# Moving the stores of what ScalarE made from the sync queue to ScalarE's DMA queue

## The chip, the cores and the metric

One core of one Trainium2 chip runs the whole kernel in one launch. The metric is the device time of that launch in microseconds (us). Engines are called as the profile calls them: PE is TensorE, ACT is ScalarE, DVE is VectorE, POOL is GpSimd, SP is SyncE, which here does nothing but issue transfers. SPq and ACTq are the instruction queues of SP and ACT.

## The reference

A bidirectional encoder block over 4096 positions and 1024 channels, in float32, one layer:

```python
xn = rmsnorm(x, norm_g)
proj = xn @ w_in                       # 4608 columns: v, x0, x1, hyena gate, lru in, lru gate
hy = dwconv3(proj[v, x0, x1])          # centred, width 3
u = v * x1
y_hy = x0 * (fftconv(u, kfilt) + skip * u)     # filter from a small sin network
xb = dwconv4(lru_in)
y_lru = rglru(xb, forward) + rglru(xb, backward)
y = concat(rmsnorm(y_hy) * silu(hy_gate), rmsnorm(y_lru) * silu(lru_gate)) @ w_out
out = rmsnorm(x + y, final_g)
```

The FFT convolution is done as matrix products: a first DFT over 128 points of the time index, a second one over 64 with twiddles in it, the product of the two spectra, and the inverse in two steps.

## The kernel before, in words

Every product is three float32r matmuls (high by high, high by low, low by high parts), so PE does most of the work. The input projection (`inproj`, L287) walks 36 blocks of 128 output columns in four passes. Within a pass it walks eight chunks of 512 positions, and each step is 24 matmuls into one of two `mm` banks of PSUM. The normalised input is kept in DRAM as `xs`, and in passes two to four `load_x` (L262) brings each chunk back as eight loads of 512 KB into 12 slots.

`consume` (L359) takes each result off PSUM. The lru input and the v, x0, x1 blocks go through `conv` (ACT and DVE). For x1 the product with v is transposed by PE in `store_u` (L339), ACT copies the result into a slot of `s4`, and a store puts it into `ut_d`: 48 pairs of block and chunk, 60 stores with the split ones at both ends (L348 to L357). A gate block is one SiLU on ACT into a slot of `cv`, and a store into `s_d`: 96 of them (L380).

Other streams are woven between the steps of the projection, in the order filter, scans, convolution:
- `phase_filter` (L473) makes the filter and its first DFT, 64 columns `j`. ACT evacuates each and a store goes to `ef_d` (L532).
- `phase_lru` (L383) loads `xb_d` in tiles of 1024 positions, makes gates (PE, ACT, DVE), scans on DVE, and stores the forward result `yf_d` and the sum `yl_d`.
- `phase_u` (L575) does the first DFT of u: 32 loads, 64 evacuations on ACT, 32 stores into `eu_d` (L600).
- `phase_mid` (L608) runs over 65 frequencies. `load` (L610) brings `ef` and `eu` for one frequency into two slots each, ACT makes the high part and POOL the low part, `tabs` (L618) loads the twiddle tables, `spectrum` multiplies, and `inverse` (L652) of the frequency before makes `r`, which is stored into `ey_d` (64 stores, L658).
- `phase_iy` (L678) does the last inverse step, 32 groups with two stores each into `yt_d` (L706).

Then `phase_out` (L710) loads the gates and branches back, normalises, projects through `w_out` and writes the output. Its tiles reuse the space of the projection's pools.

All tile dependencies become semaphores. The order of instructions in each engine's queue is written at build time by a planner that simulates the program (`schedule_with_timeline_sim=True`, L876). At run time each queue goes strictly in that order: an instruction whose semaphore has not come holds all behind it. Before the change every transfer but four loads of small parameters is issued by SP, loads and stores in one order.

Of the kernel before, what the change touches and what calls it, by code (L numbers as in the profile page):

```python
# [19 lines left out]
P = 128  # L20
L = 4096
# [4 lines left out]
TC = 512  # L26
# [85 lines left out]
def tile_hymba_block(ctx: ExitStack, tc: tile.TileContext, a: dict, out: bass.AP, dbg=None):  # L112
    nc = tc.nc
# [10 lines left out]
    s_d = [dram.tile([2, CB, P, TC], F32, name=f"sd{n}") for n in range(NCH)]  # L124
    ef_d = dram.tile([64, 2, 64, C], F32, name="efd")
    eu_d = dram.tile([64, 2, 64, C], F32, name="eud")
    ey_d = dram.tile([64, 2, 64, C], F32, name="eyd")
# [22 lines left out]
    def aux_ps():  # L150
        return pcfg["pool"].tile([P, 2, 512], F32, name="aux", bufs=pcfg["aux"])
# [29 lines left out]
    def prm(name, i):  # L181
        t, c0 = par[name]
        return t[:, c0 + i:c0 + i + 1]
# [149 lines left out]
    def store_conv(res, dst):  # L333
        y, skip, N, t0 = res
        nc.sync.dma_start(dst[:, t0 + skip:t0 + N], y[:, skip:N])
# [3 lines left out]
    def store_u(b, res):  # L339
        y, skip, N, t0 = res  # L340
        dst = ut_d[:, b * P:(b + 1) * P]
        ps = pcfg["pool"].tile([P, TC], F32, name="tp", bufs=1).rearrange("p (q c) -> p q c", c=P)
        for q in range(4):
            nc.tensor.transpose(ps[:, q, :], y[:, q * P:(q + 1) * P], ident)
        th = xpool.tile([P, 4, P], F32, name="s4", bufs=3)
        nc.scalar.activation(th, ps, AF.Copy)
        if skip:
            nc.sync.dma_start(dst[0:P - 1], th[1:, 0, :])  # L348
            nc.sync.dma_start(dst[P - 1:4 * P - 1].rearrange("(q t) c -> t q c", t=P), th[:, 1:, :])
        else:  # L350
            nc.sync.dma_start(dst[t0:t0 + TC].rearrange("(q t) c -> t q c", t=P), th)
        if N > TC:
            ps = pcfg["pool"].tile([P, TC], F32, name="tp", bufs=1).rearrange("p (q c) -> p q c", c=P)
            nc.tensor.transpose(ps[0:1, 0, :], y[:, TC:TC + 1], ident)
            th = xpool.tile([P, 4, P], F32, name="s4", bufs=3)
            nc.scalar.activation(th[0:1, 0], ps[0:1, 0], AF.Copy)
            nc.sync.dma_start(dst[L - 1:L], th[0:1, 0])  # L357

    def consume(n, e, ps):  # L359
        if 24 <= e < 30:  # L360
            i = e - 24
            store_conv(conv(n, 18 + i, ps, [prm("lcw", 6 * k + i) for k in range(4)], prm("lcb", i)), xb_d[i])
        elif e < 18:
            if 6 <= e < 12:
                r = conv(n, e, ps, [x0w[:, 6 * k + e - 6:6 * k + e - 5] for k in range(3)], x0w[:, 12 + e:13 + e])
            else:
                r = conv(n, e, ps, [prm("hcw", 18 * k + e) for k in range(3)], prm("hcb", e))
            if e < 6:
                hold[e] = r
            elif e < 12:  # L370
                store_conv(r, x0_d[e - 6])
            else:
                y, N = r[0], r[2]
                nc.gpsimd.tensor_tensor(y[:, :N], y[:, :N], hold.pop(e - 12)[0][:, :N], ALU.mult)  # L374
                store_u(e - 12, r)
        else:
            g = xpool.tile([P, TC + 8], F32, name="cv", bufs=3)
            nc.scalar.activation(g[:, :TC], ps, AF.Silu)
            r, i = (0, e - 18) if e < 24 else (1, e - 30)
            nc.sync.dma_start(s_d[n][r, i], g[:, :TC])  # L380


    def phase_lru():  # L383
# [74 lines left out]
    def mm3(ps, lhs, rhs, first=True, last=True):  # L458
        for h in range(2):
            for i, (x, y) in enumerate(((0, 0), (0, 1), (1, 0))):  # L460
                nc.tensor.matmul(ps[:, h, :NH], lhsT=lhs[:, x], rhs=rhs[:, y, h * NH:(h + 1) * NH],  # L461
                                 start=first and i == 0, stop=last and i == 2)
# [4 lines left out]
    def hv(t):  # L467
        return t[:, :, 0:NH]

    def cv2(t):  # L470
        return t.rearrange("p (h c) -> p h c", h=2)

    def phase_filter():  # L473
        with ExitStack() as st:
            hid = []
            for i in range(2):
                t = st.enter_context(tc.tile_pool(name=f"hid{i}", bufs=1)).tile([P, 2048], F32, name=f"hid{i}")
# [42 lines left out]
            for i in range(2):  # L520
                t = fw.tile([P, 2, 64], F32, name=f"lh{i}")
# [5 lines left out]
            ev = ef_d.rearrange("k r j c -> (k r) j c")  # L527
            def first_dft(j, kw, kr):
                ps = aux_ps()
                mm3(ps, fa, kr)  # L530
                nc.scalar.activation(cv2(kw), hv(ps), AF.Copy)
                nc.sync.dma_start(ev[:, j, :], kw)  # L532

            pend = None
            for j in list(range(1, 64)) + [0]:
# [15 lines left out]
                kw = fw.tile([P, C], F32, name="kw", bufs=3)  # L551
# [23 lines left out]
    def phase_u():  # L575
        JB = 2
        with tc.tile_pool(name="uu", bufs=1) as up:
            f0 = up.tile([P, P], F32, name="f0")
            nc.sync.dma_start(f0[0:64], a["c_fa"][0:64])
            nc.sync.dma_start(f0[64:], a["c_fa"][0:64])  # L580
            fu = up.tile([P, 2, P], F32R, name="fu")
            nc.vector.tensor_copy(fu[:, 0], f0)
            nc.vector.tensor_tensor(fu[:, 1], f0, fu[:, 0].bitcast(F32), ALU.subtract)
            ev = eu_d.rearrange("k r j c -> (k r) j c")
            uv = ut_d.rearrange("(p j) c -> p j c", j=64)
            for g in range(64 // JB):
                ui = up.tile([64, JB, C], F32, name="uin", bufs=3)
                nc.sync.dma_start(ui, uv[:, g * JB:(g + 1) * JB, :])
                t = up.tile([P, JB, C], F32R, name="ut", bufs=2)
                nc.vector.tensor_copy(t[0:64], ui)  # L590
                nc.vector.tensor_tensor(t[64:], ui, t[0:64].bitcast(F32), ALU.subtract)
                stg = up.tile([P, JB, C], F32, name="ustg", bufs=3)
                for j in range(JB):
                    ps = aux_ps()
                    for h in range(2):
                        for w in range(2):
                            nc.tensor.matmul(ps[:, h, :NH], lhsT=fu[:, w], rhs=t[:, j, h * NH:(h + 1) * NH],  # L597
                                             start=w == 0, stop=w == 1)
                    nc.scalar.activation(cv2(stg[:, j]), hv(ps), AF.Copy)
                nc.sync.dma_start(ev[:, g * JB:(g + 1) * JB, :], stg)  # L600
                yield WU


# [4 lines left out]
    def phase_mid():  # L608
        with tc.tile_pool(name="mid", bufs=1) as mp:
# [42 lines left out]
            def inverse(terms, s):  # L652
                ps = aux_ps()
                for m, (w, t) in enumerate(terms):
                    mm3(ps, w, t, m == 0, m == len(terms) - 1)
                o = mp.tile([P, C], F32, name="r", bufs=3)
                nc.scalar.activation(cv2(o), hv(ps), AF.Copy)
                nc.sync.dma_start(ey_d[s].rearrange("r j c -> (r j) c"), o)  # L658

            pend = None  # L660
            for k in range(64):
# [16 lines left out]
    def phase_iy():  # L678
        with tc.tile_pool(name="iy", bufs=1) as ip:
            fz = ip.tile([P, 2, P], F32, name="fz")  # L680
            nc.vector.memset(fz, 0.0)
            for i in range(2):
                nc.sync.dma_start(fz[:, i, 64 * i:64 * i + 64], a["c_fi"])
            fi = ip.tile([P, 2, 2, P], F32R, name="fi")
            nc.vector.tensor_copy(fi[:, 0], fz)
            nc.vector.tensor_tensor(fi[:, 1], fz, fi[:, 0].bitcast(F32), ALU.subtract)
            ev = ey_d.rearrange("k r j c -> (k r) j c")
            yv = yt_d.rearrange("(p j) c -> j p c", j=64)
            for g in range(32):
                e = ip.tile([P, 2, C], F32, name="e", bufs=NE)  # L690
                nc.sync.dma_start(e, ev[:, 2 * g:2 * g + 2, :])
                es = ip.tile([P, 2, 2, C], F32R, name="es", bufs=2)
                nc.scalar.activation(es[:, 0], e, AF.Copy)
                nc.vector.tensor_tensor(es[:, 1], e, es[:, 0].bitcast(F32), ALU.subtract)
                ps = aux_ps()
                for h in range(2):
                    m = 0
                    for i in range(2):
                        for fp, ep in ((0, 0), (0, 1), (1, 0)):
                            nc.tensor.matmul(ps[:, h, :NH], lhsT=fi[:, fp, i], rhs=es[:, ep, i, h * NH:(h + 1) * NH],  # L700
                                             start=m == 0, stop=m == 5)
                            m += 1
                o = ip.tile([P, C], F32, name="yo", bufs=3)
                nc.scalar.activation(cv2(o), hv(ps), AF.Copy)
                for i in range(2):
                    nc.sync.dma_start(yv[2 * g + i], o[64 * i:64 * i + 64])  # L706
                yield WI


# [170 lines left out]
```

## Time and profile before

| what | value |
|---|---|
| median of 3 runs | 2980.05 us (2979.57 to 2982.83) |
| the profiled execution's own time | 2983.15 us |
| its span, first to last instruction | 2981.2 us |
| granted TensorE clock, mean | 0.987 of full speed |
| PE busy | 2864.0 us (96%) |
| DVE, ACT, POOL busy | 2023.1, 1763.4, 832.4 us |
| DMA, mean over the span | 198 GB/s, 590.22 MB |

The time is what the runs are compared by. The span is what every other number of the profile is a part of. Busy time of DMA-issuing instructions is counted for no engine; they stand in the queues' own rows (SPq and the like). A wait names who ended it.

### The profile page before, as it was taken

What the parts mean: (1) busy time and instruction counts of PE and PEld (TensorE: products, weight loads), DVE (VectorE), ACT (ScalarE), POOL (GpSimd) and SP (SyncE); (2) the same over time, 40 slices, a digit from 0 to 9 for tenths busy, and PEclk for the clock granted to TensorE, in tenths of its full rate; (3) what the DMA queues carried; (4) which work ended last, traced back from release to release, by engine and by line L of the source; (5) the groups of instructions that cost most, each with busy time, mean ns of one, the idle gap of its engine ahead of it and who ended that gap; (6) DMA issues with size and microseconds to landing.
All of it is one profiled execution on the core that took longest, in us unless ns stands there. A gap on an engine that the chain in (4) does not pass through costs nothing.

```text
span 2981.2 us, 37289 instructions
## 1 busy us (share of the span) xinstructions
PE 2864.0 (96%) x13211; PEld 2390.1 (80%) x13211; DVE 2023.1 (68%) x2024; ACT 1763.4 (59%) x2575; POOL 832.4 (28%) x1012
## 2 busy tenths in 40 slices
PE   8999999999899898999999999999999989999998
PEld 6778888887777676777888788888888868888886
DVE  6987778657696678776666876666733366666665
ACT  4668776658697685987446667666644422222222
POOL 0013234422332323121005667766600010000001
PEclk9999999999999999999999999999999979999999
DMA  7434445434454446555986776666688665455542
GB/s 263 152 136 184 183 167 193 150 126 159 152 178 154 164 152 200 196 200 186 337 313 216 245 263 233 233 238 218 200 293 295 235 220 173 162 167 170 178 160 75
DMA packets 287352, 590.22 MB, mean 198 GB/s; under 512 B 29532, under 2 KB 150320, under 8 KB 286910
## 3 DMA queue, kind: packets, MB, share of 16 engines
q1 hardware_dynamic: 287038, 587.78, 57.2%
q8 instruction: 105, 1.72, 0.2%
q14 instruction: 81, 0.66, 0.1%
q0 software_dynamic: 128, 0.05, 0.0%
HBM read 361.24 MB, written 226.49 MB: 197 GB/s over the span
## 4 chain that ended last, share of the span: by engine, by line
PE 60%; ACT 13%; DVE 10%; DMA 8%; issue 6%; POOL 3%; SPq 1%; ACTq 0%; POOLq 0%; DVEq 0%
PE mm L302 11%; PE mm L304 11%; PE mm L303 11%; PE aux L461 9%; PE aux L785 4%; PE aux L783 4%; PE aux L784 4%; PE aux L700 2%; DMA eu<-eud 2%; DVE cv L330 2%; PE aux L597 2%; DVE sy L762 2%; ACT L433 1%; ACT L421 1%; ACT aa L424 1%
## 5 line engine op out<-in xcount | busy, mean ns | idle before, releaser
L302 PE MATMUL mm<-x,w 128*128 128x512 f32 x2304 | 911.9, 397 | 15.7 <-DMA x<-xs 6.6
L303 PE MATMUL mm<-x,w 128*128 128x512 f32 x2304 | 910.5, 395 | 0.0
L304 PE MATMUL mm<-x,w 128*128 128x512 f32 x2304 | 907.0, 394 | 0.0
L302 PEld LDWEIGHTS mm<-x,w 128*128 128x128 f32 x2304 | 436.0, 189 | 108.6 <-DMA x<-xs 10.0
L304 PEld LDWEIGHTS mm<-x,w 128*128 128x128 f32 x2304 | 435.9, 189 | 85.7 <-issue 0.5
L303 PEld LDWEIGHTS mm<-x,w 128*128 128x128 f32 x2304 | 436.2, 189 | 83.3 <-issue 1.9
L330 DVE SCALAR_TENSOR_TENSOR cv<-raw,cols,cv 128x512 f32<-128x512 f32 (+2 forms) x336 | 270.3, 807 | 117.2 <-ACT cv L328 112.1
L783 PE MATMUL aux<-w,A 128*128 128x512 f32 x768 | 304.7, 399 | 9.9 <-ACT w L728 9.9
L784 PE MATMUL aux<-w,A 128*128 128x512 f32 x768 | 304.7, 397 | 1.4 <-DVE w L729 1.4
L785 PE MATMUL aux<-w,A 128*128 128x512 f32 x768 | 304.7, 400 | 0.0
L764 POOL CAST sr<-sy 128x256 fp32r<-128x256 f32 x32 | 36.4, 1138 | 740.0 <-DVE sy L762 495.2
L615 POOL TENSOR_TENSOR ef<-ef 128x768 fp32r<-128x768 f32 x64 | 125.6, 1962 | 236.2 <-DMA ef<-efd 181.1
L419 PE MATMUL aux<-hl,wg 128*128 128x512 f32 x576 | 156.9, 401 | 24.8 <-DVE hl L412 11.2
L320 ACT ACTIVATE raw<-mm 128x512 f32<-128x512 f32 x192 | 113.5, 591 | 109.7 <-PE mm L304 109.4
L783 PEld LDWEIGHTS aux<-w,A 128*128 128x128 f32 x768 | 145.8, 190 | 40.7 <-ACT w L728 10.6
L374 POOL TENSOR_TENSOR cv<-cv 128x512 f32<-128x512 f32 (+1 forms) x48 | 73.1, 1523 | 369.6 <-DVE cv L330 354.6
L784 PEld LDWEIGHTS aux<-w,A 128*128 128x128 f32 x768 | 145.7, 190 | 34.8 <-DVE w L729 2.9
L785 PEld LDWEIGHTS aux<-w,A 128*128 128x128 f32 x768 | 145.9, 190 | 31.0
L757 ACT ACTIVATE y<-y 128x1536 f32<-128x1536 f32 x32 | 47.7, 1489 | 204.8 <-DVE S L756 187.1
L456 DVE TENSOR_TENSOR rs<-r,rs 128x768 fp32r<-128x768 f32 x65 | 94.5, 1453 | 94.9 <-ACT rs L455 94.9
L419 PEld LDWEIGHTS aux<-hl,wg 128*128 128x128 f32 x576 | 107.6, 190 | 61.3 <-DVE hl L412 17.4
L615 POOL TENSOR_TENSOR eu<-eu 128x768 fp32r<-128x768 f32 x64 | 125.3, 1957 | 30.4 <-ACT eu L614 30.4
(193 smaller groups left out, 5220.0 us busy)
## 6 DMA issues: line engine op xcount, KB each, us to landing
x<-xs SPq DMA_DIRECT2D x192, 512.0 KB
xs<-x SPq DMA_DIRECT2D x64, 512.0 KB
efd<-kw SPq DMA_DIRECT2D x64, 384.0 KB
xb<-xbd SPq DMA_DIRECT2D x48, 512.0 KB
sd<-cv SPq DMA_DIRECT2D x96, 256.0 KB
eud<-ustg SPq DMA_DIRECT2D x32, 768.0 KB
ef<-efd SPq DMA_DIRECT2D x64, 384.0 KB
eu<-eud SPq DMA_DIRECT2D x64, 384.0 KB
```

The costliest lines, as they stand in the source:

```text
L302: nc.tensor.matmul(ps, lhsT=w[:, 0, kt, :], rhs=x[kt][:, 0], start=kt == 0, stop=False)
L303: nc.tensor.matmul(ps, lhsT=w[:, 0, kt, :], rhs=x[kt][:, 1], start=False, stop=False)
L304: nc.tensor.matmul(ps, lhsT=w[:, 1, kt, :], rhs=x[kt][:, 0], start=False, stop=kt == KT - 1)
L320: nc.scalar.activation(R[:, K - 1:K - 1 + TC], ps, AF.Copy)
L330: nc.vector.scalar_tensor_tensor(y[:, :N], R[:, k:k + N], w[k], y[:, :N], op0=ALU.mult, op1=ALU.add)
L419: nc.tensor.matmul(ps[:, h], lhsT=wg[:, u, 2 * d + gi, :], rhs=v[:, hs], start=i == 0, stop=i == 2)
L456: nc.vector.tensor_tensor(dst[:, 1], src, dst[:, 0].bitcast(F32), ALU.subtract)
L461: nc.tensor.matmul(ps[:, h, :NH], lhsT=lhs[:, x], rhs=rhs[:, y, h * NH:(h + 1) * NH], start=first and i == 0, stop=last and i == 2)
L615: eng.tensor_tensor(t[:, 1], raw, t[:, 0].bitcast(F32), ALU.subtract)
L783: nc.tensor.matmul(ps[:, h], lhsT=ht, rhs=w[:, 0, sl], start=b == 0, stop=False)
L784: nc.tensor.matmul(ps[:, h], lhsT=ht, rhs=w[:, 1, sl], start=False, stop=False)
L785: nc.tensor.matmul(ps[:, h], lhsT=lt, rhs=w[:, 0, sl], start=False, stop=b == CB - 1)
```

## The change

The eight store instructions whose source tile was written by ACT are issued with `nc.scalar.dma_start` in place of `nc.sync.dma_start`. The loads, and the stores of what DVE or POOL made, stay on SP. Sizes, slots and arithmetic are the same. The planner orders the queues anew.

```diff
@@ store_u
         if skip:
-            nc.sync.dma_start(dst[0:P - 1], th[1:, 0, :])
-            nc.sync.dma_start(dst[P - 1:4 * P - 1].rearrange("(q t) c -> t q c", t=P), th[:, 1:, :])
+            nc.scalar.dma_start(dst[0:P - 1], th[1:, 0, :])
+            nc.scalar.dma_start(dst[P - 1:4 * P - 1].rearrange("(q t) c -> t q c", t=P), th[:, 1:, :])
         else:
-            nc.sync.dma_start(dst[t0:t0 + TC].rearrange("(q t) c -> t q c", t=P), th)
+            nc.scalar.dma_start(dst[t0:t0 + TC].rearrange("(q t) c -> t q c", t=P), th)
...
-            nc.sync.dma_start(dst[L - 1:L], th[0:1, 0])
+            nc.scalar.dma_start(dst[L - 1:L], th[0:1, 0])
@@ consume
-            nc.sync.dma_start(s_d[n][r, i], g[:, :TC])
+            nc.scalar.dma_start(s_d[n][r, i], g[:, :TC])
@@ phase_filter, first_dft
-                nc.sync.dma_start(ev[:, j, :], kw)
+                nc.scalar.dma_start(ev[:, j, :], kw)
@@ phase_u
-                nc.sync.dma_start(ev[:, g * JB:(g + 1) * JB, :], stg)
+                nc.scalar.dma_start(ev[:, g * JB:(g + 1) * JB, :], stg)
@@ phase_mid, inverse
-                nc.sync.dma_start(ey_d[s].rearrange("r j c -> (r j) c"), o)
+                nc.scalar.dma_start(ey_d[s].rearrange("r j c -> (r j) c"), o)
@@ phase_iy
-                    nc.sync.dma_start(yv[2 * g + i], o[64 * i:64 * i + 64])
+                    nc.scalar.dma_start(yv[2 * g + i], o[64 * i:64 * i + 64])
```

## Rows read from the trace of the kernel before

**Rows 1.** The page, engines: busy us, share of the span, instructions.
```profile
PE 2864.0 (96%) x13211; PEld 2390.1 (80%) x13211; DVE 2023.1 (68%) x2024; ACT 1763.4 (59%) x2575; POOL 832.4 (28%) x1012
```

**Rows 2.** Busy time by stretch: length, busy us of each engine, clock, DMA.
```profile
220.00:690.00 470.00, 470.00 (x2324) 410.18 (x2324) 332.70 (x433) 336.41 (x583) 164.66 (x388) 1.00 0.46 166
690.00:1400.00 710.00, 657.37 (x2843) 525.53 (x2842) 542.46 (x446) 572.49 (x744) 196.64 (x126) 0.98 0.51 175
...
1640.00:2170.00 530.00, 513.92 (x2430) 440.86 (x2429) 380.46 (x344) 358.33 (x477) 356.82 (x353) 1.00 0.68 235
```

**Rows 3.** SP's own waits, 690 to 1400: us in total, times, longest.
```profile
SPq L442 <- DVE bb L441: 154.3, 24, 10.6
...
SPq L351 <- ACT s L346: 61.0, 21, 8.1
...
SPq L380 <- ACT cv L378: 16.6, 7, 5.2
...
SPq L266 <- PE mm L304: 8.8, 19, 2.6
```

**Rows 4.** SP's own waits, 1640 to 2170.
```profile
SPq L658 <- ACT r L657: 108.9, 42, 6.1
SPq L620 <- POOL ib L625: 94.5, 41, 5.1
SPq L380 <- ACT cv L378: 60.3, 30, 4.4
...
SPq L266 <- PE mm L304: 6.4, 15, 1.0
```

**Rows 5.** SP's queue in order of time, 1900 to 1917: start, us.
```profile
1912.99 0.32 SPq L658 DMA_DIRECT2D eyd<-r  x1
1913.41 0.38 SPq L613 DMA_DIRECT2D ef<-efd  x1
```

**Rows 6.** ACT's waits, 1640 to 2170.
```profile
ACT eu L614 <- DMA eu<-eud: 78.3, 37, 6.2
...
ACT ef L614 <- DMA ef<-efd: 34.5, 27, 3.5
```

**Rows 7.** DMA issues from 690 to 1400: count and KB each.
```profile
utd<-s SPq DMA_DIRECT2D x31, 256.0 KB
...
sd<-cv SPq DMA_DIRECT2D x9, 256.0 KB
...
utd<-s SPq DMA_DIRECT2D x5, 0.5 KB
```

**Rows 8.** Two lines' issue instructions: duration in ns, least, median, most.
```profile
L351 SPq DMA_DIRECT2D utd<-s x42: 365/371/797, 150.5 to 1196.7; - x42
...
L380 SPq DMA_DIRECT2D sd<-cv x96: 319/320/924, 1223.4 to 2380.0; - x96
```

**Rows 9.** ACT in order of time, 400 to 440: two neighbours.
```profile
418.56 0.81 ACT L531 ACTIVATE kw<-aux 128x768 f32<-128x768 f32 x1
419.25 0.95 ACT L546 ACTIVATE win<-absd,tn 128x768 f32<-128x768 f32 x1
```

**Rows 10.** The chain that ended last, 690 to 1400, share of it by line.
```profile
by line: issue 12.3%; DVE cv L330 6.1%; ACT L433 5.0%; ACT L421 4.4%; PE mm L302 4.4%; PE mm L304 4.3%; ACT aa L424 4.3%; PE mm L303 4.3%; ACT th L421 4.0%; ACT m L427 4.0%; DMA x<-xs 4.0%; DVE bb L429 3.5%; ACT th L425 3.2%; ACT m L433 3.2
```

**Rows 11.** PE's waits, 690 to 1400.
```profile
PE tp L344 <- POOL cv L374: 13.7, 4, 5.8
PE aux L419 <- DVE hl L412: 11.2, 11, 2.3
...
PE mm L302 <- DMA x<-xs: 6.6, 5, 3.5
```

**Rows 12.** The same chain, two of its transfers: start, us.
```profile
973.40 2.64 DMA yfd<-bb
...
2380.05 5.25 DMA sd<-cv
```

**Rows 13.** SP's own waits over the whole run, one ended by a load.
```profile
SPq L600 <- DMA x<-xs: 8.8, 6, 2.6
```

## The prediction

> **What bounds the kernel now.** I read the engines' busy times first, then the busy times by stretch, and then, for the stretches in which PE isn't full, who waited for whom. PE is busy 96% of the span [rows 1]. The stretches tell where the other 4% are [rows 2]. From 220 to 690 (filter) PE is busy all 470 us. From 1400 to 1640 (first DFT of u) and from 2170 to 2360 (last inverse step) it is the same: full, with no wait of PE listed. No queue order can speed these up; they can only lose. PE idles 52.6 us of the 710 from 690 to 1400 (the scans) and 16.1 us of the 530 from 1640 to 2170 (the middle of the convolution) [rows 2]. So what the change can give sits in these two stretches and at the seam near 2380, where the output phase takes over; what it can cost sits wherever ACT is near full.
>
> What holds the loads is seen in SP's own waits. SP takes its transfers in one fixed order, so a store that waits for ACT keeps back every load behind it. In the middle stretch the longest waits of SP are for ACT's `r` (108.9 us in 42 waits) and, third, for ACT's gate (60.3) [rows 4]. One place shows the pattern: the store of `r` goes out at 1912.99, and the load of `ef` directly behind it, 0.42 us after it starts [rows 5]. ACT in turn idles 78.3 and 34.5 us there for `eu` and `ef` [rows 6].
>
> **Part one: 380 issues leave SP.** By the loops these are 60 + 96 + 64 + 32 + 64 + 64 stores. An issue takes 0.320 us for the gates and 0.371 for the transposed u [rows 8], so at least 380 x 0.320 = 122 us of issuing leave SP. I value this at nothing by itself: SP spends its time in waits, and what covers the issues is the same waits. At worst it stays nothing.
>
> **Part two: loads that stood behind the stores.** In the middle stretch SP's listed waits sum to 321.9 us (seven rows, the first and the last of them shown). Of these 108.9 + 60.3 = 169.2 us, 53%, go away from SP [rows 4]. If the 16.1 us of idle PE [rows 2] fall in proportion, that is -8.5 us. The ends are 0 (the `eu` load stays behind the table load, whose wait for POOL, 94.5 us, stays [rows 4]) and -16.1. I take the proportion, because the `ef` load is the one released.
>
> In the scans SP's listed waits sum to 535.9 us (eleven rows); 61.0 + 16.6 = 77.6 us of them, 14.5%, go [rows 3]. The largest, for the forward scan's `bb`, stays. The waits of PE that begin with late loads are 13.7 (the product on POOL, queued behind loads of `hf`), 11.2 (low part of `xb`) and 6.6 (x) [rows 11], 31.5 us in sum; 14.5% of it is -4.6 us. The ends are 0 and -31.5; the share going is small, so I stay with it.
>
> **Part three: the last gate store.** At the seam the chain runs through the store of the last gate, 5.25 us from issue to landing, behind loads of the output phase on the same queue. A store of twice its size that stood alone took 2.64 us [rows 12]. On a queue of its own I give it that: -2.6 us, with 0 as the other end. [...]
>
> **Part four: what ACT pays.** A store on ACT's queue stands behind the activation that made its data and needs its end. Two neighbours on ACT overlap now: one starts at 418.56 and takes 0.81, the next starts at 419.25, 0.12 us before the first one's end [rows 9]. With a store between them that overlap goes and the issue comes in: 0.320 + 0.12 = 0.44 us for most, 0.371 + 0.12 = 0.49 for u. The trace has no issue on ACT; the nearest rows are these of SP. Below, it could be nothing, where ACT idles behind the store anyway.
>
> In the scans there are 31 + 9 + 5 such stores [rows 7]: 31 x 0.49 + 14 x 0.44 = 21.4 us. ACT is busy 572.49 of 710 us there [rows 2], the fullest it gets in any long stretch, and seven of the entries in the chain are ACT's: 5.0 + 4.4 + 4.3 + 4.0 + 4.0 + 3.2 + 3.2 = 28.1% [rows 10]. So 28.1% of 21.4, +6.0 us; ends 0 and +21.4. Queued behind a held ACT are the tanh and square root of the gates, and DVE's scan waits for these.
>
> In the middle stretch 60 + 51 stores at 0.44 make 48.8 us. I cost this at nothing: ACT idles 78.3 + 34.5 = 112.8 us for loads there [rows 6], more than twice that, and this idle time covers it. Without the cover it costs up to 48.8 us.
>
> In the three full stretches the 64 + 32 + 64 stores and the gates there are covered by PE's own work; ACT is busy 336.41 of 470 us in the first [rows 2]. One cost has no row of ACT: SP's stores sometimes wait for a load that they do not read, 8.8 us in six waits at L600 [rows 13]. So transfers share semaphores, and such a wait would now hold ACT. I take 0, because PE keeps some steps of PSUM ahead; the upper end is four lines at 8.8 us each, +35.
>
> **The sum.** -8.5 - 4.6 - 2.6 + 6.0 = -9.7 us. The profiled execution took 2983.15 us (span 2981.2 and 1.95 around it), so its like would take 2973.5. It lies 3.1 us above the median of the runs, 2980.05, from which the forecast is taken: 2970.4 us. What can be told from no change is about 0.2%, 6 us.
>
> **The rivals.** *ACT becomes the bound.* The holds in the two stretches sum to 21.4 + 48.8 = 70.2 us. The gains of parts two and three sum to 15.7. From 21.7 us of holds on the path (31% of them) the kernel is slower by over 6 us; at half it is +35.1 - 15.7 = +19.4, 2999.5 us. For it: ACT's 81% in the scans [rows 2], and 28% of the chain without any store in it [rows 10]. Against it: the idle time of rows 6.
>
> *Nothing moves.* The loads held by a store were early enough. PE is full in three stretches, and the 16.1 us of the middle come from the products of spectra, not from `ef`. Holds and gains then cancel: 2980, between 2974 and 2986. [...]
>
> The planner's new order can move each case by some microseconds either way; that is why neither gain nor loss gets more than half of the chance.
>
> **How the numbers follow.** Gain: 0.42, at 2970, own range 2954 to 2974 (the lower end has the middle's whole 16.1, the seam's 2.6 and 7 of the scans' 31.5, with holds that cost nothing). Nothing moves: 0.27. ACT as the bound: 0.31, at 2999.5, from 2986 up; the part over 3008 (over 62% of the holds on the path) I give 0.1, below 2954 another 0.07. So the range is 2954 to 3008, and faster, same, slower are 0.42, 0.27, 0.31.
>
> **What would show it.** Right: SP's waits at L351, L380, L532 and L658 gone; `ef` loads issued without a wait for ACT; ACT's waits for `ef` shorter; PE idle in 1640 to 2170 under 10 us; the last gate store landing in under 3.5 us; ACT's idle time in the scans shorter by some 20 us. Wrong: waits of ACT for transfers that its next work does not need, or PE waits for ACT's `th`, `bb` or `cv` growing from 690 on; an order of the projection's steps that differs so much that stretches no longer match.

## The result, and the profile after

The changed kernel takes 3007.3 us in the median of 4 runs (3005.6 to 3011.79), the kernel before on the same chip 2981.31 (2979.57 to 2982.83). The ratio is 1.009, 95% interval 1.0074 to 1.0106: some 27 us slower, where 10 us faster were forecast. The profiled execution's span is 3003.7 us against 2981.2.

The page's engine line of the kernel after. Against [rows 1], ACT gains 1.6 us and PE 5.8, for the same 13211 matmuls, on a span 22.5 longer; the mean granted clock is 0.986 against 0.987. Most of the growth is therefore idle time of PE.

```profile
PE 2869.8 (96%) x13211; PEld 2390.3 (80%) x13211; DVE 2026.2 (67%) x2024; ACT 1765.0 (59%) x2575; POOL 834.3 (28%) x1012
```

The same kernel by stretch, with the columns of [rows 2]. The last line is the kernel before from 1400 to 1640.

```profile
220.00:690.00 470.00, 470.00 (x2326) 410.44 (x2325) 331.97 (x434) 337.96 (x583) 157.32 (x386) 1.00 0.47 167
690.00:1400.00 710.00, 650.81 (x2809) 518.61 (x2808) 532.56 (x440) 569.85 (x738) 203.13 (x125) 0.98 0.51 173
1400.00:1640.00 240.00, 237.58 (x1113) 204.26 (x1113) 151.31 (x136) 113.17 (x196) 35.42 (x37) 1.00 0.80 276
1640.00:2170.00 530.00, 506.70 (x2374) 432.33 (x2373) 388.65 (x344) 359.65 (x480) 364.18 (x357) 0.99 0.66 227
```

```profile
1400.00:1640.00 240.00, 240.00 (x1133) 208.07 (x1132) 156.30 (x140) 120.80 (x206) 40.13 (x42) 1.00 0.83 280
```

PE's idle time grew from 52.6 to 59.2 us in the scans, from 0 to 2.4 from 1400 to 1640, and from 16.1 to 23.3 in the middle of the convolution, by 16.2 us in all. Read the counts beside the busy times. From 220 to 690 nothing is lost (2326 matmuls against 2324). In the scans PE gets through 2809 matmuls where it got through 2843, from 1400 to 1640 through 1113 (1133 before), in the middle of the convolution through 2374 (2430): 34 + 20 + 56 = 110 fewer. Matmuls of the projection follow each other at 0.23 us here (227 ns from start to start, the median of either trace), so that is about 25 us, as an estimate, and the span grew by 22.5. Most of the loss, 90 of the 110, is in the two stretches in which gain was looked for.

PE's waits of the kernel after, 690 to 1400 (us in total, times, longest). Among those that grew against the kernel before are that for `hl` (from 11.2 to 14.2, [rows 11]), that for a gate's `cv` (from 3.0 to 4.8) and that for `bb` (from 1.9 to 3.7). The second fence has the last two of the kernel before.

```profile
PE aux L419 <- DVE hl L412: 14.2, 12, 2.6
...
PE mm L302 <- ACT cv L378: 4.8, 2, 2.4
...
PE aux L419 <- ACT bb L421: 3.7, 10, 1.1
```

```profile
PE mm L302 <- ACT cv L378: 3.0, 1, 3.0
...
PE aux L419 <- ACT bb L421: 1.9, 8, 0.3
```

PE's longest wait from 1640 to 2170 is for the product of spectra (`rs`, made by DVE): first of the kernel after, then of the kernel before.

```profile
PE aux L461 <- DVE rs L456: 10.2, 17, 1.6
```

```profile
PE aux L461 <- DVE rs L456: 6.6, 11, 1.1
```

SP's waits of the kernel after, first 690 to 1400, then 1640 to 2170. The waits at L351, L380 and L658 of [rows 3, 4] are gone as announced. But the time SP waited did not go. All its waits together are 586 us in the scans (567 before) and 425 in the middle (372 before): there the table load's wait for POOL's `ib` alone is 231.7 us, 94.5 before.

```profile
SPq L442 <- DVE bb L441: 170.9, 23, 10.6
SPq L409 <- DVE bb L429: 168.1, 38, 20.6
...
SPq L266 <- PE mm L304: 17.7, 21, 4.6
```

```profile
SPq L620 <- POOL ib L625: 231.7, 45, 9.2
SPq L613 <- PE aux L461: 67.5, 34, 5.7
```

ACT's waits of the kernel after in the middle: both waits for loads are shorter than in [rows 6], by 6.2 and 9.1 us, and PE idles more all the same.

```profile
ACT eu L614 <- DMA eu<-eud: 72.1, 32, 5.2
...
ACT ef L614 <- DMA ef<-efd: 25.4, 12, 3.7
```

ACT and its queue in order of time, after. The gate's activation ends at 1311.55; the store's issue takes 0.33 us; the table load after it starts 0.38 us after that end. With no store between them, the next activation (it ends at 1314.29) and the table load behind it are 0.01 us apart.

```profile
1310.95 0.60 ACT L378 ACTIVATE cv<-mm 128x512 f32<-128x512 f32 x1
1311.58 0.33 ACTq L380 DMA_DIRECT2D sd<-cv  x1
1311.93 1.28 ACT L433 ACT_TABLE_LOAD   x1 [0.39 <-ACT cv L378]
1313.23 1.06 ACT L433 ACTIVATE m<-m 128x1024 f32<-128x1024 f32 x1
1314.30 1.28 ACT L421 ACT_TABLE_LOAD   x1
```

The order of the queues was planned anew, and that is much more than the moved stores. For each engine: the instructions that both programs have in its queue, and the fewest of them that must change place to turn the one order into the other.

```
PE    13179 instructions, 1713 of them change place
DVE    2024                 98
ACT    2358                218
POOL   1012                 92
SP     1250                 79   (the transfers that stay on SP)
```

### The profile page after: what moved, and what is told of

It is laid out like the page before. It is cut to its first block, busy times and chain, and to the rows that moved or that the text cites. A ratio compares the mean times of both kernels' runs of the same rounds, so it can differ in the third digit from the quotient of the medians.

```text
span 3003.7 us, 37110 instructions
## 1 busy us (share of the span) xinstructions
PE 2869.8 (96%) x13211; PEld 2390.3 (80%) x13211; DVE 2026.2 (67%) x2024; ACT 1765.0 (59%) x2575; POOL 834.3 (28%) x1012
## 5 line engine op out<-in xcount | busy, mean ns | idle before, releaser
L764 POOL CAST sr<-sy 128x256 fp32r<-128x256 f32 x32 | 34.5, 1080 | 747.2 <-DVE sy L762 510.2
L419 PE MATMUL aux<-hl,wg 128*128 128x512 f32 x576 | 159.6, 405 | 27.0 <-DVE hl L412 14.2
```

Source lines behind the costliest of these rows:

```text
L419: nc.tensor.matmul(ps[:, h], lhsT=wg[:, u, 2 * d + gi, :], rhs=v[:, hs], start=i == 0, stop=i == 2)
```

## Experiments: the order or the queue

**Order and queue apart.** The theory: the time went into the new order of instructions, above all PE's, and not into the queue. The rival: into the queue, through holds of ACT and shared semaphores. An order can be held: after tracing, an edge without a semaphore is added from each instruction to the next one of a recorded order, so that the planner must write that order. The places of the transfers in the queues of SP and ACT stay the planner's. `ORDER` is the recorded order, as packed numbers of instructions. That a queue runs in its planned order shows in the traces of before and after: numbered by the two recorded orders, ACT's 2358 activations agree one by one in line, tiles and shape.

```diff
+def pin_order(tc, engines):
...
+    info = mybir.DependencyInfo(mybir.DependencyClass.NoSync, mybir.DependencyReason.DATA)
+    for e in engines:
+        names = np.cumsum(np.frombuffer(zlib.decompress(base64.b85decode(ORDER[e])), "<i4")).tolist()
+        for a, b in zip(names, names[1:]):
+            tc.add_manual_dep(traced[b], f"I-{a}", info, reason="order")
...
     with tile.TileContext(nc, schedule_with_timeline_sim=True) as tc:
         tile_hymba_block(tc, args, out)
+        pin_order(tc, ('PE', 'DVE', 'Pool', 'Activation'))
```

First, the kernel before with all stores on SP, its four computing engines held to the changed kernel's order:

> All stores back on SP's queue, but PE, DVE, POOL and ACT work through their instructions in exactly the order that the planner wrote for the changed kernel. Theory A, the planner's new order costs the time: about 3003 us, as slow as the changed kernel (+22 us or more). Theory B, the queue itself costs it (ACT held by its stores, loads and stores that wait for each other's semaphores): about 2981 us, the time of the kernel before.

Then the changed kernel's stores on ACT with the order of the kernel before:

> All 380 stores on ACT's queue as in the change, but PE, DVE, POOL and ACT's activations keep exactly the order of the kernel before, and SP's loads all but exactly. Theory A, the new order: about 2981 us or some microseconds less, since the loads no longer stand behind the stores (the forecast of part two, up to -16). Theory B, the queue itself: 3003 us or more, with waits of ACT behind its own stores in the scans (21 us of holds) and the middle (49 us).

And the same with PE alone held to the order of before (`pin_order(tc, ('PE',))`):

> All stores on ACT's queue; only PE keeps the order of the kernel before, ACT, DVE, POOL and SP have what the planner writes for them with the stores on ACT. Theory A1, PE's own order (how many steps of the projection stand between a frequency's second DFT and its inverse) carries the cost of the new plan: about 2987 us, within 0.2% of before. Theory A2, the orders of ACT and DVE carry it: about 3000 us or more.

| kernel | median us | before, same chip | ratio, 95% interval |
|---|---|---|---|
| order of after, stores on SP | 3004.39 | 2986.72 | 1.0063 (1.0048 to 1.0077) |
| order of before, stores on ACT | 2987.44 | 2986.72 | 1.0002 (0.9992 to 1.0011) |
| PE's order of before, stores on ACT | 2989.64 | 2982.63 | 1.0018 (1.0007 to 1.0029) |

The order alone, without a store moved, costs 0.63%, 19 us by the ratio. All 380 stores on ACT's queue cost nothing that can be told when the order of before is held. PE's order accounts for most: with it alone restored, and the other engines planned around it, 0.9% becomes 0.18%. What is left between 0.63% and 0.9% (1.009/1.0063 = 1.0027, 8 us, the two intervals put together reach from about 1.0005 to 1.0049) belongs to the queue in that order.

The traces hint at where. In the order of after, PE idles 51.8 us in the scans with the stores on SP (the line below) and 59.2 with the stores on ACT; in the middle it is 22.9 and 23.3. So the loss of the middle is there without a moved store, and that of the scans seems to come with the queue. This is one execution of each, and their spans differ by only 2.2 us.

```profile
690.00:1400.00 710.00, 658.19 (x2823) 524.87 (x2822) 534.91 (x442) 572.80 (x741) 203.81 (x125) 0.97 0.50 173
```

The middle stretch, 1640 to 2170, of these three, in the order of the table: PE 507.07 us and 2390 matmuls, as in the kernel after, then 514.49 and 516.42, as before.

```profile
1640.00:2170.00 530.00, 507.07 (x2390) 430.77 (x2389) 386.44 (x347) 357.65 (x478) 367.19 (x359) 1.00 0.66 228
```

```profile
1640.00:2170.00 530.00, 514.49 (x2439) 443.89 (x2438) 385.57 (x348) 362.83 (x481) 363.42 (x356) 0.99 0.68 237
```

```profile
1640.00:2170.00 530.00, 516.42 (x2450) 445.95 (x2449) 388.70 (x351) 365.43 (x486) 367.64 (x359) 0.99 0.68 235
```

The kernel with the order of before and its stores on ACT is the clean test of the change itself. SP's waits in its middle stretch:

```profile
SPq L620 <- POOL ib L625: 181.1, 47, 6.6
SPq L613 <- PE aux L461: 121.2, 46, 7.5
```

The 169.2 us of waits behind stores are gone, and the loads wait for themselves instead: the table load for POOL to be done with the slot (94.5 before), the loads of `ef` and `eu` (both L613) for PE to be done with theirs (23.6 before). The loads that came to the head of the queue sooner met slots that weren't free: these two waits grew from 118.1 to 302.3 us together. ACT's wait for `ef` is halved there, and PE idles 15.5 us against 16.1:

```profile
ACT eu L614 <- DMA eu<-eud: 68.2, 31, 7.3
...
ACT ef L614 <- DMA ef<-efd: 16.2, 10, 3.6
```

**One group of stores at a time, planned freely.** Only the change to L380 is left in the first, only that to L658 in the second.

```diff
-            nc.sync.dma_start(s_d[n][r, i], g[:, :TC])
+            nc.scalar.dma_start(s_d[n][r, i], g[:, :TC])
```

> Only the 96 gate stores on ACT's queue, everything planned anew. PE's order departs from the kernel before after the gates begin (about 1223 us) and the middle's median distance from second DFT to inverse falls from 10.4 to 9.9 us of PE work. Theory A (the order): some 8 us lost from 1200 to 1400 and some 8 in the middle, 2996 to 3003 us. Theory B (holds of ACT by these 96 stores at 0.44 us, up to 42 us of them, a third on the path): the same time, but with ACT's own stores as what PE's waits lead back to; A would show them led back to DVE and to positions in the order.

```diff
-                nc.sync.dma_start(ey_d[s].rearrange("r j c -> (r j) c"), o)
+                nc.scalar.dma_start(ey_d[s].rearrange("r j c -> (r j) c"), o)
```

> Only the 64 stores of the inverse's result on ACT's queue, everything planned anew. The order is that of the kernel before up to the middle stretch, there the median distance falls from 10.4 to 9.7 us of PE work. Theory A: nothing until 1600 us, then some 10 us lost in the middle: about 2992 us. If the order is only a matter of luck and not of this distance: no loss, 2980 to 2986.

The gates alone: 3002.04 us against 2982.63, ratio 1.0059 (1.0045 to 1.0073). The `r` stores alone: 2990.26, 1.0026 (1.0017 to 1.0035). The 96 gate stores, a quarter of those moved, bring two thirds of the loss, and with them 1401 instructions of PE change place, where all the stores move 1713. Of the two losses expected, some 8 us each, the middle's shows (PE idles 25.1 us there, 16.1 before), and that from 1200 to 1400 us only in part (17.4 us against 14.6). As theory A has it, PE's longest wait in the middle leads back to DVE:

```profile
PE aux L461 <- DVE rs L456: 16.2, 24, 1.5
```

The `r` stores lose less than the 10 us expected in the middle (18.8 us of idle PE against 16.1), though their plan has the same median distance, 9.7 us, as the changed kernel. That already speaks against the distance as the cause.

**New plans without a moved store.** Is this loss what the planner does to a store on ACT's queue, or what any new plan does here? Two small shifts of the weave, each with the stores on SP and on ACT. The first also moves one step of the projection over the border of two stretches, so it isn't a new plan alone; the second is nearer to that.

```diff
-X2 = 28
+X2 = 29
```

> All stores on SP as before; X2 is 29 in place of 28, so one step of the projection moves from the convolution's stretch to the scans', and the planner writes a new order. Theory A (the change lost time because its new order happened to be a worse one; the order of the kernel before is a good draw): this order loses too though no queue changed, 2988 to 3005 us, and in the middle stretch more waits of PE for the product of spectra than the 6.6 us before. Theory B (the planner orders badly because it takes a store on ACT for cheap): within 0.2% of the kernel before, 2976 to 2988.

> The same shift of one step, with all the stores on ACT, planned freely. Theory A: another draw, within 0.3% of its twin with the stores on SP (the queue itself gave 0.02% and 0.2% when the order was held). Theory B: slower than its twin by 0.6 to 0.9%, about 3005 us or more.

```diff
-S2 = 1.0
+S2 = 1.01
```

> All stores on SP; the weight of the scans in the weave (S2) is 1.01 in place of 1, which shifts their steps a little against the projection's. Theory A: not the order of before, so slower by 0.2 to 0.8%, 2988 to 3005. Theory B: within 0.2% of the kernel before.

> The same weight with all stores on ACT, planned freely. Theory A: within 0.3% of its twin on SP. Theory B: slower than its twin by 0.6 to 0.9%.

| weave | stores on SP | stores on ACT | ACT over SP |
|---|---|---|---|
| X2 = 29 | 1.0104 (1.0087 to 1.0121) | 1.0126 (1.0111 to 1.0142) | 1.0022 |
| S2 = 1.01 | 1.0023 (1.0013 to 1.0034) | 1.0051 (1.0036 to 1.0066) | 1.0028 |
| as it was | 1 | 1.0090 (1.0074 to 1.0106) | 1.0090 |

Both new plans lose with no queue changed, 0.23% and 1.04% (2988.96 and 3011.28 us against 2983.77). So a plan other than the one of before costs time without a moved store; the 1.04% is as much as the whole change cost, but part of it may be the step that was moved. Theory B of these expectations falls; A holds, save that the first shift costs more than its 2988 to 3005. Each twin on ACT is 0.2 to 0.3% over its twin on SP, the same size as the 0.27% above. The twins' orders differ too, and for the first pair the two intervals put together reach down to no difference.

The middle stretch of the first shift with its stores on SP; it stands beside that of the kernel after, 26 us of PE idle.

```profile
1640.00:2170.00 530.00, 504.08 (x2360) 427.19 (x2359) 388.96 (x343) 356.32 (x476) 366.64 (x355) 0.99 0.66 227
```

**What in the order does it?** In the planned order of before, 10.4 us of PE work (median over the frequencies, by the durations of the traces) lie between a frequency's second DFT and its inverse; in that of the changed kernel 9.7. The theory: too little work there to cover the product on DVE. The edit, made on a held order of PE, keeps the six matmuls of an inverse together and moves them behind the projection's matmuls that follow them. The lines show the pattern of one frequency: `mm` is the projection, `ef` and `eu` the two DFTs, `rs` the inverse. Only PE is held here; the other engines are planned anew around it, and no run holds the changed kernel's own order of PE without the edit.

```diff
-PE: eu x6, mm x10, rs x1, mm x5, rs x5, mm x2, ef x6
+PE: eu x6, mm x10, mm x5, mm x2, rs x6, ef x6
```

> The changed kernel, its stores on ACT, with PE held to the changed kernel's own order but for one edit: in the middle of the convolution the six matmuls of each frequency's inverse are kept together and moved behind the projection's matmuls that follow them (up to eight), so that the median PE work planned between a frequency's second DFT and its inverse goes from 9.7 to 11.0 us (10.4 in the kernel before). Theory A (part of the loss is that the new order leaves the product of spectra too little time): PE's waits for that product in the middle fall from 10.2 to under 5 us, and the time from 3007 to between 2996 and 3002. Rival (those waits only show where PE happens to stand still): the idle time goes to other waits, 3004 to 3010.

> The kernel before, all stores on SP, with PE held to its own order but for the same edit: the median distance goes from 10.4 to 11.7 us. Theory A: the 6.6 us of waits for the product fall under 3, and the time goes to between 2975 and 2980, faster than both kernels. Rival: unchanged, 2980 to 2990, PE waiting for something else in the same places.

This theory falls. The changed kernel's order with the edit: 3017.69 us against 2986.03, 1.0097 (1.0083 to 1.011), no better than 1.009 and above both forecasts, and PE waits for the product 19.8 us, not under 5:

```profile
PE aux L461 <- DVE rs L456: 19.8, 23, 2.5
```

The order of before with the edit: 2987.05 us, 1.0 (0.999 to 1.001), PE's waits for the product 10.5 us where 6.6 stood. More planned distance went with a longer wait in both, so the distance does not explain the loss. Why the product came later still is not shown. Which feature of the order costs the time stays open.

**A load taken off SP as well.** The order of before, all stores on ACT, and the table load issued from POOL:

```diff
-                nc.sync.dma_start(raw, a["c_tabs"][:, k])
+                nc.gpsimd.dma_start(raw, a["c_tabs"][:, k])
```

> The order of the kernel before with all stores on ACT, and the 65 table loads of the middle stretch issued from POOL's queue, so that loads of ef and eu stand behind no wait for POOL on SP's queue. If the gain of the freed loads was eaten by the table load standing next (SP's wait for POOL grew from 94.5 to 181.1 us when the stores left): up to 10 us faster than with the table loads on SP, 2976 us. If the loads' own slots bound them, or PE never waited for these loads: no change, 2987 us.

3000.26 us against 2982.63, 1.0055 (1.0043 to 1.0068), slower than both forecasts. SP, freed of that wait too, waits for the next slots instead, and PE now waits for POOL, for the low part of `ef` and for the table itself (6.3 us). The first row is SP's, the second PE's, 1640 to 2170.

```profile
SPq L613 <- PE aux L461: 350.5, 97, 11.3
```

```profile
PE aux L461 <- POOL ef L615: 7.8, 6, 2.1
```

No kernel tried beats the kernel before.

## Why the prediction was wrong

**The step that failed** is the sentence "The planner's new order can move each case by some microseconds either way": a term that the sum left at nothing. By the ratios it measured +19 us in this plan, and +7 and +31 in two other plans that moved no store. All four parts were worked out as if the order stayed, and with the order held they come to 0.02% together, under 1 us (the interval is about -2 to +3), where -9.7 was forecast. Two of the prediction's signs of being wrong showed in the profile: PE's waits for `cv` and `bb` grew, and the orders differ widely.

That 3007.3 us lies inside the stated range, just under its end at 3008, is luck. That end was worked out from ACT's holds, 62% of 70.2 us of them on the path, and the holds measured 15.4 us in all (part four).

**Part one** (380 issues leave SP, nothing): agrees with the held order.

**Part two** (-8.5 in the middle, -4.6 in the scans) was wrong by itself too. With the order held, PE idles 530 - 514.49 = 15.5 us in the middle, 16.1 before, and 710 - 656.54 = 53.5 in the scans, 52.6 before. The share of 53% was taken of SP's seven longest rows; of all its waits in the middle, 372 us, it is 45%. And the proportion took SP's waits for time that loads lose. With the stores gone from SP and the order held, the loads waited for their slots: all of SP's waits in the middle were 435 us, where 372 stood. The ends at 0 were right. The sign "ACT's waits for `ef` shorter" came true (34.5 to 16.2 us with the order held, 25.4 in the kernel after) and told nothing of the time, for PE's idle time fell by no more than 0.6 us with it.

**Part three** (-2.6 at the seam): the chain of the kernel after still runs through the last gate store, and from ACT's queue it took 5.88 us, not under 3.5. The second line is from the order of before with the stores on ACT.

```profile
2399.57 5.88 DMA sd<-cv
```

```profile
2384.61 5.01 DMA sd<-cv
```

The term of -2.6 was an estimate from one store that stood alone, and no run shows it. On ACT's queue, beside the loads of the output phase, 5.25 us became 5.88 in the one and 5.01 in the other: no gain near 2.6.

**Part four** (+6.0 in the scans) had the price of one store about right, 0.44 us, and the number of stores that pay it wrong. Before a table load the price is 0.38 - 0.01 = 0.37 us, at the place shown above; before an activation ACT idles 0.46 us in the median of 37, which with the lost overlap of 0.12 [rows 9] makes 0.58, as an estimate. But of the 45 stores in the scans only 15 held ACT, for 5.8 us where 21.4 were forecast, and of the 107 in the middle 22, for 9.6 us where 48.8 were taken as the most. These are ACT's waits that ended with an instruction of its own; the longest of each stretch:

```profile
ACT L433 <- ACT cv L378: 1.9, 5, 0.4
```

```profile
ACT ef L614 <- ACT cv L378: 5.1, 11, 0.5
```

Of the 380 stores 210 go out while ACT is already in a later activation, as this one of `r`:

```profile
1743.88 0.79 ACT L638 ACTIVATE ha<-aux 64x768 f32<-64x768 f32 x1
1744.01 0.33 ACTq L658 DMA_DIRECT2D eyd<-r  x1
```

The 28.1% that was to fall on the path did not show with the order held. In the three planned orders the queue adds 0.2 to 0.3%, 7 to 8 us; holds of ACT and the shared semaphores are both candidates, and no run separates them. That semaphores are shared does show: in the trace of the kernel after, eight of them tell of the landing of 1630 transfers, the stores of ACT's queue and the transfers of SP's alike, and loads of `x` on SP wait for stores of ACT's queue whose data and slots they don't use, here over the whole run.

```profile
SPq L266 <- DMA utd<-s: 23.2, 1, 23.2
SPq L266 <- DMA sd<-cv: 12.4, 5, 5.9
```

**The rivals.** "ACT becomes the bound" gave 2999.5, near the result for the wrong reason: the order of before with the stores on ACT has the holds, 12.6 us of them in the two stretches, and no loss. "Nothing moves" was right about the change in the order of before: 2987.44 against 2986.72 us.

## What to carry to other kernels

Where a planner writes the order, an edit to one queue can be an edit to all of them: here 380 moved stores changed the place of 1713 instructions of PE. Before a gain or a loss is given to the edit, hold the old order and run the edit, hold the new order without it, and shift something harmless as a control. Ask also how a kernel's neighbours in order do: here both were slower, by 0.23% and 1.04%. And look whether the slot behind is free before a wait in a queue that only issues transfers is given a worth: here 169.2 us of SP's waits went with the stores, the loads behind them waited for their slots, and PE's idle time in the middle fell by 0.6 us.

## What the runs showed of the hardware

The issue of a gate store took about as long on ACT as on SP: 326 ns in the median of 96 against 320 [rows 8]; the longest took 1005 against 924. What the stores cost ACT differed from one to the next: 46 of the 380 left ACT idle, 19.1 us in all, and 210 went out while it was in a later activation.

```profile
L380 ACTq DMA_DIRECT2D sd<-cv x96: 321/326/1005, 1226.4 to 2399.6; - x96
```
